# A two-layer decoder trunk on one core: the second layer's p projection in the convolution's end, attention's end on TensorE in a written order

## The chip, the core and the metric

The kernel runs on one core of one Trainium2 chip. The core has five engines that run side by side and wait for one another through semaphores: TensorE (PE, matmuls; PEld is its weight load), VectorE (DVE), ScalarE (ACT), GpSimd (POOL), and SyncE (SP, which here only issues transfers). PE writes its results to PSUM, eight banks of 128 x 512 float32. The metric is the device time of one execution in microseconds (us). Durations of single steps come from the trace of one profiled execution.

## What is computed

A trunk of two layers over 512 tokens of width 1024, all in float32. Layer 0 has a causal Conformer convolution, layer 1 differential attention with 8 heads; each is followed by a SwiGLU feed-forward and by a gated embedding of its own input p (256 features per layer):

```python
for i in range(DEPTH):                      # DEPTH = 2
    if i % N_MIXERS == 0:
        u = rms_norm(h, conv_norm_g[j])
        h = h + conformer_conv(u, ...)      # pw1, gate, 31 depthwise taps, layer norm, silu, pw2
    else:
        u = rms_norm(h, attn_norm_g[j])
        h = h + diff_attention(u, ...)      # heads' outputs, normalised, @ w_o
    u = rms_norm(h, ffn_norm_g[i])
    h = h + swiglu(u, ffn_w_gate[i], ffn_w_up[i], ffn_w_down[i])
    gate = jax.nn.sigmoid(rms_norm(h, ple_norm_g[i]) @ ple_w_gate[i])
    h = h + gate * (p[i] @ ple_w_proj[i])
```

The product `p[i] @ ple_w_proj[i]` depends on the inputs alone: it can be computed at any time before the last line of its layer. `w_o` is a 1024 x 1024 matrix: each of its eight output chunks sums over the eight heads.

## The kernel before

**Layout.** Activations lie as eight chunks of 128 channels by 512 tokens (`h[0]` to `h[7]`). Each float32 product is made from three matmuls of operands that are split into a high and a low part (`mm3`, L161: low x high, high x low, high x high). A weight tile is 128 x 1024: `weight()` (L145) loads it on SP's queue into the ring `wraw` (two buffers), ACT makes the high part `whi` (L156), DVE the low part `wlo` (L158); `whi` and `wlo` have four buffers each. PSUM has three rings: `mm` (four banks), `sc` (two), `tp` (two).

**Who sets the order.** A scheduler orders the instructions of each engine ahead of the run, by the order in which the program names them and by its own model of time; then each engine runs its list in order. `tc.issue_after(x)` keeps the instructions of a block behind x if they are on x's engine. Within `tc.manual_schedule(engines=...)` the named engines keep the order in which the program is written.

**The convolution's end (L482 to L544).** After the last chunk's taps (L482), `moments` (L415) squares the chunks y[5], y[6] and y[7] on ACT (L424) and adds them up on DVE or POOL (L428, L430). `project` (L269) makes one chunk of the first layer's p projection: six matmuls into an `mm` bank and a copy by ACT (L275). `factor` (L490) calls it: four chunks behind the last tap, then the sums over channels on PE (`add_moments`, L432, narrow matmuls L436 and wide ones L437), two chunks, then the row of scales (L513 to L522: DVE, POOL, ACT, PE), two chunks. With the scales each y is normalised (L539), passed through silu (L540) and split (L542, L544) for the matrix pw2 (`linear`, L546 and L571), whose first three weights are loaded in this time.

**Attention's end (L1015 to L1080).** The work of head hd and block qb of 128 queries is cut into three stages: `stage_s` (scores on PE, L944, L945; minimum, exponential and the difference of the two softmaxes on DVE and ACT, L947 to L956), `stage_t` (transposes on PE, L964, split L966, L967) and `stage_a` (product with the values, L980, L981; with the head's last block the head's normalisation, L987 to L1002). They stand in the list `stages`: in turn n, the score stage of unit n, the transposes of unit n - 2, the product of unit n - 3. 63 of the 96 stages are given out between the matmuls of the q, k and v slabs (L1028); 33 are left. `unit_end` (L896) transposes the last q and k block for the last two heads. `stage_o` (L1006) transposes a finished head and splits it (`split_scaled`, L177 and L178) into `ot[hd]`.

Then the second layer's features are loaded and split (`pfeatures`, L257 and L1055), its projection is computed with a stage from the list after each half chunk (L1057 to L1068), and the output matrix follows with further stages between (L1080): `linear` takes each chunk over all eight heads, the first two chunks side by side, `heads_until` (L1070) giving out stages until the head that is next is done. `add_attn` (L1076) adds a finished chunk to h and prepares it for the feed-forward (`Norm.chunk`: split L177 and L178, square L196, sum on POOL L197).

Of the kernel before, what the change touches and what calls it, by code (L numbers as in the profile page):

```python
# [12 lines left out]
F32 = mybir.dt.float32  # L13
F32R = mybir.dt.float32r
# [6 lines left out]
P = 128  # L21
S = 512
# [50 lines left out]
HALVES = slice(0, DH), slice(DH, P)  # L73
LT = 2
LA = 3
SQ_ACT = True
# [15 lines left out]
def trunk(ctx, tc, xT, pT, wts, diag, dww, vec, rel, onehot, lamv, out):  # L92
# [77 lines left out]
    def both(t):  # L170
        return t[:, 0], t[:, 1]
# [85 lines left out]
    def pfeatures(layer, parts):  # L257
        for k, (hi, lo) in enumerate(parts):
            raw = sb([P, 1024], "wraw", 2)[:, :S]
            nc.sync.dma_start(raw, pT[layer, :, k * S : (k + 1) * S])  # L260
            A.copy(hi, raw)
            (G if layer == 0 else V).tensor_tensor(lo, raw, f(hi), ALU.subtract)
# [4 lines left out]
    last_product = [None]  # L267

    def project(ph, m, w, o, step=lambda: None):  # L269
# [5 lines left out]
        A.copy(o, acc)  # L275
        return o
# [162 lines left out]
    for c in range(NC):  # L439
# [9 lines left out]
        if c > 0:  # L449
# [33 lines left out]
    other_taps(NC - 1)  # L483
    for c in range(NC - 3, NC):
        moments(c)


    pp = []

    def factor(after):  # L490
        m = len(pp)
        if m < 6:
            o = sb([P, S], f"D{m}", 1)
        elif m == 6:
            pw.append(sb([P, 2, S], "C4", 2))
            o = pw[2][:, 0]
        else:
            o = pw[2][:, 1]
        with tc.issue_after(after[0].ins):
            pp.append(project(ph, m, pw[m // 4], o))  # L500

    pw = [weight(), weight()]
# [18 lines left out]
    with tc.issue_after(last_product[0].ins):  # L521
        last_product[0] = T.matmul(lrow, ones, dg, start=True, stop=True)  # L522
    for _ in range(2):
        factor(last_product)
    with tc.issue_after(last_pow[0].ins):
# [502 lines left out]
    for what, at, pace in QKV:  # L1028
        ws = slab(GLO if at > 0 else 0)
        for tb in range(4):  # L1030
# [7 lines left out]
            else:  # L1038
                waiting = unit(at, ws, tb, between)
    unit_end(*waiting)  # L1040


    done = [0]

    def step():
        if stages:
            n, s = stages.pop(0)
            s()
        else:
            n = 99  # L1050
        while done[0] < NH and (n - LA - 3) // 4 > done[0]:
            stage_o(done[0])
            done[0] += 1

    ph = pfeatures(1, [both(sb([P, 2, S], t, 2, F32R)) for t in ("C0", "C1")])  # L1055
    pp = []
    for m in range(NC):  # L1057
        if m % 4 == 0:
            w = weight()
        step()  # L1060
        if m < 2:
            o = sb([P, S], f"D{m + 2}", 1)
        elif m % 2 == 0:
            o2 = sb([P, 2, S], f"C{m // 2 + 1}", 2)
            o = o2[:, 0]
        else:
            o = o2[:, 1]
        pp.append(project(ph, m, w, o, step))  # L1068

    def heads_until(k):  # L1070
        while done[0] <= k:
            step()

# [5 lines left out]

    linear(NC, ot, add_attn, 2, heads_until, step)  # L1080
    n2 = Norm("ple_g1")
# [34 lines left out]
def _layout(a):  # L1116
# [20 lines left out]

    tiles += proj(0)
    tiles += list(_stationary(a["conv_w_pw2"][0]))
    tiles += ffn(0)  # L1140
    tiles += list(_stationary(a["ple_w_gate"][0]))
    qkv = a["attn_w_qkv"][0]
    for what, at, _ in QKV:
# [7 lines left out]
        tiles += list(_moving(slab))  # L1151
    tiles += proj(1)
    tiles += list(_stationary(a["attn_w_o"][0]))
# [61 lines left out]
```

## Time and profile before

| | us |
|---|---|
| median of three executions | 1282.84 |
| the three executions | 1288.49, 1282.84, 1282.57 |
| the profiled execution's own time | 1285.64 |
| its span in the trace | 1283.8 |

| stage in the profiled execution | from, us | to, us |
|---|---|---|
| last taps end, first projection begins | 148.08 | |
| pw2's matmuls run without a break | 178.48 | |
| last tokens' matmul of q, k and v begins | 790.34 | |
| last score stage's minimum ends on DVE | | 833.66 |
| output matrix: last addition into h begins | 885.24 | |

How to read the profile: the page gives each engine's busy time over the span; a view by windows gives the same for chosen stretches, with the clock that PE was granted (1.00 is full) and the share of DMA; a timeline lists one engine's instructions by start and duration, with the idle time before an instruction and what ended it in brackets (`[1.04 <-DVE C L917]`: 1.04 us idle, ended by the instruction of L917 on DVE that writes the tile C). L158 is line 158 of the kernel. A busy PE can run at half clock, so the clock's column belongs to every statement about PE.

### The profile page before, as it was taken

The page shows a single profiled execution, that of the slowest core. Times are in us where ns is not written, and L with a number is a line of the kernel's source. Part 1 is how long each engine was busy: PE and PEld are TensorE (multiplying, and loading weights), DVE is VectorE, ACT ScalarE, POOL GpSimd, SP SyncE. Part 2 cuts the span into 40 slices and gives each one's busy share as a digit, 9 for nine tenths or more (in the row PEclk, how much of TensorE's full clock was granted, in tenths as well). Part 3 has the DMA queues.
Part 4 walks back from the last instruction along what each step waited for, and adds up shares of the span by engine and source line. Part 5 has one row for each costly group of instructions (what it writes and reads, how often), then busy time and mean ns, then how long its engine had stood idle before and what let it go on. Part 6 is the DMA issues. An engine that isn't in the chain of part 4 may idle for free. (4 is left out here: it accounts for less than half of the span.)

```text
span 1283.8 us, 18407 instructions
## 1 busy us (share of the span) xinstructions
PE 1253.2 (98%) x7056; PEld 1089.0 (85%) x7056; DVE 910.9 (71%) x1470; ACT 614.0 (48%) x1019; POOL 273.5 (21%) x239
## 2 busy tenths in 40 slices
PE   8999899999999999999999998999999999999998
PEld 5888678889899989988788886778888899899887
DVE  6888646785578557776678897946974588558665
ACT  5542445443255325454566766834542355235442
POOL 4645323000000000033335544122000001000030
PEclk8999989999999999999999999999999999999999
DMA  6654313275457545233222221313364466444241
GB/s 236 223 163 158 114 48 115 70 209 142 117 143 187 151 119 137 70 121 101 77 92 87 85 76 51 94 49 120 118 169 139 122 176 173 138 110 118 79 140 66
DMA packets 60164, 157.32 MB, mean 123 GB/s; under 512 B 6403, under 2 KB 11011, under 8 KB 60076
## 3 DMA queue, kind: packets, MB, share of 16 engines
q1 hardware_dynamic: 53344, 135.94, 33.2%
q0 software_dynamic: 4608, 16.78, 8.0%
q10 hardware_dynamic: 2124, 3.43, 0.9%
q8 instruction: 55, 0.90, 0.3%
q14 instruction: 33, 0.27, 0.1%
HBM read 151.91 MB, written 4.21 MB: 122 GB/s over the span
## 5 line engine op out<-in xcount | busy, mean ns | idle before, releaser
L164 PE MATMUL mm<-A,whi 128*128 128x512 f32 (+1 forms) x904 | 312.7, 347 | 0.6 <-DVE A L178 0.3
L163 PE MATMUL mm<-A,wlo 128*128 128x512 f32 (+1 forms) x904 | 308.3, 346 | 4.5 <-DVE wlo L158 2.5
L165 PE MATMUL mm<-A,whi 128*128 128x512 f32 (+1 forms) x904 | 310.0, 344 | 0.0
L156 ACT CAST whi<-wraw 128x1024 fp32r<-128x1024 f32 (+2 forms) x150 | 151.2, 1014 | 233.0 <-PE mm L165 93.4
L158 DVE TENSOR_TENSOR wlo<-wraw,whi 128x1024 fp32r<-128x1024 f32 (+2 forms) x146 | 186.6, 1280 | 65.8 <-ACT whi L156 65.0
L163 PEld LDWEIGHTS mm<-A,wlo 128*128 128x128 f32 x904 | 171.8, 190 | 27.5 <-DVE wlo L158 4.2
L164 PEld LDWEIGHTS mm<-A,whi 128*128 128x128 f32 x904 | 172.1, 190 | 24.5 <-DVE A L178 3.8
L165 PEld LDWEIGHTS mm<-A,whi 128*128 128x128 f32 x904 | 172.1, 190 | 20.4 <-issue 1.0
L164 PE MATMUL mm<-B,whi 128*128 128x512 f32 x352 | 137.3, 391 | 0.0
L650 POOL DMA_DIRECT2D C<-in_wts x32 | 28.1, 880 | 511.4 <-DVE h L761 179.4
L165 PE MATMUL mm<-B,whi 128*128 128x512 f32 x352 | 137.1, 390 | 0.0
L163 PE MATMUL mm<-B,wlo 128*128 128x512 f32 x352 | 134.9, 392 | 0.0
L197 POOL TENSOR_TENSOR acc<-acc,wk 128x512 f32<-128x512 f32 x42 | 65.7, 1564 | 229.6 <-ACT wk L196 122.1
L761 DVE TENSOR_TENSOR h<-mm,h 128x512 f32<-128x512 f32 x48 | 33.0, 687 | 64.8 <-PE mm L165 64.8
L165 PEld LDWEIGHTS mm<-B,whi 128*128 128x128 f32 x352 | 66.1, 188 | 14.4
L163 PEld LDWEIGHTS mm<-B,wlo 128*128 128x128 f32 x352 | 66.1, 188 | 14.0
L164 PEld LDWEIGHTS mm<-B,whi 128*128 128x128 f32 x352 | 66.1, 188 | 13.9
L165 PE MATMUL mm<-whi,A 128*128 128x512 f32 x192 | 75.7, 395 | 0.0
L164 PE MATMUL mm<-wlo,A 128*128 128x512 f32 x192 | 74.9, 395 | 0.0
L163 PE MATMUL mm<-whi,A 128*128 128x512 f32 x192 | 74.8, 396 | 0.0
L222 POOL TENSOR_TENSOR r<-v,mhalf 128x8 f32<-128x8 f32 (+1 forms) x31 | 46.2, 1490 | 117.1 <-DVE v L220 94.6
L643 DVE TENSOR_TENSOR wlo<-wraw,whi 128x1024 fp32r<-128x1024 f32 x32 | 39.2, 1225 | 32.8 <-ACT whi L642 32.8
(269 smaller groups left out, 2700.7 us busy)
## 6 DMA issues: line engine op xcount, KB each, us to landing
wraw<-in_wts SPq DMA_DIRECT2D x162, 512.0 KB, 3.7
C<-in_wts SPq DMA_DIRECT2D x32, 512.0 KB, 4.7
C<-in_wts POOLq DMA_DIRECT2D x32, 512.0 KB, 6.2
bias<-in_wts SPq DMA_DIRECT2D x32, 256.0 KB, 3.8
wraw<-in_wts SPq DMA_DIRECT2D x16, 384.0 KB, 3.1
D<-in_diag SPq DMA_DIRECT2D x22, 256.0 KB, 4.2
C<-in_diag SPq DMA_DIRECT2D x16, 256.0 KB, 4.4
h<-in_xT SPq DMA_DIRECT2D x8, 256.0 KB, 5.2
```

The source lines that it names most:

```text
L156: A.copy(hi[:, cut], raw[:, cut])
L158: eng.tensor_tensor(lo[:, cut], raw[:, cut], f(hi[:, cut]), ALU.subtract)
L163: T.matmul(acc, al, bh, start=first, stop=False)
L164: T.matmul(acc, ah, bl, start=False, stop=False)
L165: return T.matmul(acc, ah, bh, start=False, stop=last)
L197: self.last = self.eng.tensor_tensor(self.acc, self.acc, sq, ALU.add)
L222: last_pow[0] = G.tensor_tensor(r[:, :n], v[:, :n], mhalf[:, :n], ALU.pow)
L643: V.tensor_tensor(lo, raw, f(hi), ALU.subtract)
L650: nc.gpsimd.dma_start(q, wts[i + 2].rearrange("p (a s) -> p a s", a=2), accum_op=ALU.add)
L761: V.tensor_tensor(h[m], acc, h[m], ALU.add)
```

## The change

It has two parts.

**The second layer's p projection moves into the convolution's end.** At the fourth chunk of the convolution (c == 3) the second layer's features are loaded and split, their low parts on POOL, into the buffers `bias` and `C4`. `factor` gets a second list: eight more chunks, of the second layer, whose results go from a `big` buffer to device memory through ACT's queue (`kept`). The order on PE becomes: six chunks of the first layer, one of the second, the moments, four of the second, the row of scales, three of the second, the last two of the first. The squares of y[6] and y[7] are kept behind the copies of the fourth and sixth chunk on ACT (`last_copy`). Before the second layer's gated embedding the eight kept chunks are loaded back on SP's queue.

**Attention's end is written out for PE.** The last `unit_end` and all that follows stand in a `manual_schedule` block for PE. `step()` gives out one stage, and in every third call at most one `stage_o`. `filling()` is the first pass of the output matrix: for each chunk the four products with heads 0 to 3, one product (three matmuls) after each stage, then an addition into h. Nine stages come before `unit_end` (`AHEAD`). When the stages are used up, the rest of the first pass runs, then the second pass over heads 4 to 7: six chunks side by side in four `mm` and two `sc` banks for heads 4, 5 and 6, then head 7 for each of them with `add_attn`, then the last two chunks. `two_halves` loads the weights of two chunks for four heads as one 128 x 1024 tile.

The diff, cut to its core:

```diff
-            (G if layer == 0 else V).tensor_tensor(lo, raw, f(hi), ALU.subtract)
+            G.tensor_tensor(lo, raw, f(hi), ALU.subtract)
...
+        if c == 3:
+            ph1 = pfeatures(1, [[sb([P, S], "bias", 2, F32R) for _ in range(2)], both(sb([P, 2, S], "C4", 2, F32R))])
...
-    for c in range(NC - 3, NC):
-        moments(c)
+    moments(NC - 3)
...
+        with tc.issue_after(after.ins):
+            project(ph1 if second else ph, m, (pw1 if second else pw)[m // 4], o)
+        if second:
+            kept = dram.tile([P, S], F32, tag=f"pp{m}", name=f"pp{m}")
+            nc.scalar.dma_start(kept, o)
+            o = kept
+        made.append(o)
...
+    pw, pw1 = [[weight(), weight()] for _ in range(2)]
     for _ in range(4):
-        factor(last_tap)
+        factor(last_tap[0])
+    with tc.issue_after(last_copy[0].ins):
+        moments(NC - 2)
+    for _ in range(2):
+        factor(last_product[0])
+    with tc.issue_after(last_copy[0].ins):
+        moments(NC - 1)
+    factor(last_product[0], True)
     with tc.issue_after(last_product[0].ins):
         add_moments(y[NC - 1], sums["sq"], True, False)
         add_moments(macc, sums["acc"], False, True)
-    for _ in range(2):
-        factor(last_moment)
+    for _ in range(4):
+        factor(last_moment[0], True)
...
+    for _ in range(3):
+        factor(last_product[0], True)
     for _ in range(2):
-        factor(last_product)
+        factor(last_product[0])
...
-    unit_end(*waiting)
...
-        while done[0] < NH and (n - LA - 3) // 4 > done[0]:
+        count[0] += 1
+        if done[0] < NH and (n - LA - 3) // 4 > done[0] and count[0] % 3 == 2:
             stage_o(done[0])
             done[0] += 1
...
+    def filling():
+        for m in range(NC):
+            if m % 2 == 0:
+                two = two_halves(m, 0)
+            w = two[m % 2]
+            acc = mm()
+            for k in range(4):
+                while done[0] <= k:
+                    yield
+                mm3(acc, wpart(w, k), ot[k], k == 0, k == 3)
+                if k == 3:
+                    V.tensor_tensor(h[m], acc, h[m], ALU.add)
+                yield
+
+    fill = filling()
+    with tc.manual_schedule(engines={T.engine}):
+        for _ in range(AHEAD):
+            step()
+            next(fill)
+        unit_end(*waiting)
+        while stages:
+            step()
+            next(fill, None)
+        for _ in fill:
+            step()
+        while done[0] < 7:
+            step()
+        ws = [w for m in range(0, 6, 2) for w in two_halves(m, S)]
+        accs = [mm() for _ in range(4)] + [sc() for _ in range(2)]
+        for w, acc in zip(ws, accs):
+            for k in range(3):
+                mm3(acc, wpart(w, k), ot[4 + k], k == 0, False)
+        while done[0] < NH:
+            step()
+        for m, (w, acc) in enumerate(zip(ws, accs)):
+            mm3(acc, wpart(w, 3), ot[7], False, True)
+            add_attn(m, acc)
+        for m, w in zip((6, 7), two_halves(6, S)):
+            acc = mm()
+            for k in range(4):
+                mm3(acc, wpart(w, k), ot[4 + k], k == 0, k == 3)
+            add_attn(m, acc)
...
-    linear(NC, ot, add_attn, 2, heads_until, step)
```

The weights' order in memory follows: the second layer's two projection tiles now stand behind the first layer's.

More of the change, by code (lines that the diff above doesn't have):

```diff
@@ L274, in project @@
             step()
-        A.copy(o, acc)
+        last_copy[0] = A.copy(o, acc)
         return o
@@ L1048, in step, with add_attn @@
             s()
[L1049 to L1051 removed]
+        count[0] += 1
+        if done[0] < NH and (n - LA - 3) // 4 > done[0] and count[0] % 3 == 2:
             stage_o(done[0])
             done[0] += 1
[L1055 removed]
+    norm = Norm("ffn_g1")
+    def add_attn(m, acc):
+        V.tensor_tensor(h[m], acc, h[m], ALU.add)
+        norm.chunk(m)
+    base = wnext[0]
@@ new lines, in trunk, with two_halves @@
+    wnext[0] += NC
+    def two_halves(m, first):
+        raw = sb([P, 2, S], "wraw", 2)
+        nc.sync.dma_start(raw, bass.AP(wts.tensor, wts.offset + (base + m) * P * 1024 + first, [[1024, P], [P * 1024, 2], [1, S]]))
+        raw = raw.rearrange("p a s -> p (a s)")
+        hi = sb([P, 1024], "whi", 4, F32R)
+        lo = sb([P, 1024], "wlo", 4, F32R)
+        A.copy(hi, raw)
+        V.tensor_tensor(lo, raw, f(hi), ALU.subtract)
+        return [tuple(t[:, k * S : (k + 1) * S] for t in (hi, lo)) for k in range(2)]
@@ L1064, in trunk @@
             o2 = sb([P, 2, S], f"C{m // 2 + 1}", 2)
[L1065 to L1072, printed above, removed]
-    norm = Norm("ffn_g1")
-    def add_attn(m, acc):
-        V.tensor_tensor(h[m], acc, h[m], ALU.add)
-        norm.chunk(m)
-    linear(NC, ot, add_attn, 2, heads_until, step)
+        if m >= 2:
+            o = o2[:, m % 2]
+        nc.sync.dma_start(o, later[m])
+        pp.append(o)
     n2 = Norm("ple_g1")
```

31 lines of the change are left out of this document (17 added, 14 removed).

## The prediction

> **What bounds the kernel now.** I read the page's table of engines first. One core, so there is one span.
>
> ```profile
> PE 1253.2 (98%) x7056; PEld 1089.0 (85%) x7056; DVE 910.9 (71%) x1470; ACT 614.0 (48%) x1019; POOL 273.5 (21%) x239
> ```
>
> TensorE (PE) is busy for 1253.2 of 1283.8 us. The change computes the same matmuls, so it can win only idle PE time (30.6 us in all) and time in which PE runs at a lower clock. Next I read the table by windows over the two stages that the change touches: the convolution's end (first four rows) and attention's end up to the output matrix's last matmul (last four; 849 to 862 is left out). Its columns are busy time and instructions of each engine, then clock, DMA share and GB/s.
>
> ```profile
> 125.60:148.00 22.40, 22.31 (x123) 17.25 (x122) 11.40 (x16) 10.16 (x15) 7.41 (x7) 1.00 0.52 164
> 148.00:158.70 10.70, 7.44 (x26) 5.30 (x25) 9.33 (x13) 2.61 (x5) 5.29 (x5) 0.84 0.16 49
> 158.70:168.20 9.50, 9.50 (x37) 7.95 (x37) 0.97 (x5) 2.24 (x4) 0.02 (x1) 0.50 0.20 55
> 168.20:178.50 10.30, 9.52 (x31) 6.45 (x29) 6.00 (x8) 6.32 (x13) 7.28 (x6) 0.80 0.00 0
> ...
> 791.40:803.50 12.10, 5.86 (x28) 4.62 (x27) 11.83 (x32) 9.37 (x22) 4.53 (x5) 0.73 0.34 110
> 803.50:826.00 22.50, 20.57 (x110) 16.90 (x108) 21.05 (x58) 18.38 (x44) 4.10 (x5) 0.92 0.44 129
> 826.00:849.00 23.00, 22.79 (x135) 19.83 (x134) 13.63 (x40) 10.65 (x26) 3.89 (x4) 1.00 0.11 36
> ...
> 862.00:885.00 23.00, 23.00 (x102) 19.00 (x103) 14.98 (x15) 12.69 (x18) 9.51 (x6) 1.00 0.52 160
> ```
>
> Two things to see. From 158.7 to 168.2 PE is 9.50 of 9.50 us busy, but at a granted clock of 0.50: that "busy" hides half a stall. And from 791.4 to 826 VectorE (DVE) is busy 11.83 + 21.05 of 34.6 us, 95%, while PE idles: there DVE sets the pace, so PE's idle time can't all be had by reordering PE. Last I read PE's timeline for the idle time in attention's end.
>
> ```profile
> 793.74 0.63 PE L899 MATMUL tp<-ident,big 128*128 128x128 f32 x4 [1.04 <-DVE C L917]
> 795.19 0.30 PE L944 MATMUL sc<-C,C 128*128 128x128 f32 x1 [0.82 <-DVE st L947]
> 797.92 0.47 PE L944 MATMUL sc<-C,C 128*128 128x128 f32 x1 [1.65 <-DVE st L947]
> 801.13 0.66 PE L944 MATMUL sc<-C,C 128*128 128x384 f32 x1 [2.52 <-DVE st L955]
> 811.77 0.44 PE L944 MATMUL sc<-C,C 128*128 128x384 f32 x1 [0.81 <-DVE st L947]
> 815.27 0.47 PE L944 MATMUL sc<-C,C 128*128 128x512 f32 x1 [0.94 <-DVE st L947]
> 857.13 1.20 PE L163 MATMUL mm<-A,wlo 128*128 128x512 f32 x4 [0.78 <-ACT A L177]
> 861.90 0.50 PE L163 MATMUL mm<-A,wlo 128*128 128x512 f32 x1 [1.75 <-DVE wlo L158]
> ```
>
> These waits add up to 10.3 us, all on DVE or ACT results. PE had nothing else there: the weights of projection and output matrix are issued only from 796.62 on, when the features' splits (L262) have let go of the load ring.
>
> ```profile
> 796.62 15.12 SPq L153 DMA_DIRECT2D wraw<-in_wts  x6
> ```
>
> **The change, part by part.** *Price of a matmul.* The second and third of the next rows are 16 matmuls apart, so one 128x512 matmul costs (152.37 - 148.71) / 16 = 0.229 us at full clock. The second layer's projection is 8 chunks of 6, 48 matmuls: 11.0 us. The output matrix is 8 x 8 x 3 = 192 matmuls, 44 us, in either kernel.
>
> ```profile
> 148.08 0.80 PE L163 MATMUL mm<-wth,wlo 128*128 128x512 f32 x1
> 148.71 0.39 PE L164 MATMUL mm<-wth,whi 128*128 128x512 f32 x1
> ...
> 152.37 0.39 PE L165 MATMUL mm<-wtl,whi 128*128 128x512 f32 x1
> 156.01 0.79 PE L163 MATMUL mm<-wth,wlo 128*128 128x512 f32 x1 [3.26 <-ACT D L275]
> 158.74 1.73 PE L436 MATMUL tp<-ones,wk 128*128 128x1 f32 x8
> ...
> 168.22 1.42 PE L163 MATMUL mm<-wth,wlo 128*128 128x512 f32 x1
> ...
> 172.41 0.40 PE L165 MATMUL mm<-wth,whi 128*128 128x512 f32 x1
> ...
> 173.33 1.02 PE L522 MATMUL tp<-wk,ones 128*128 128x512 f32 x2
> ...
> 178.48 0.50 PE L163 MATMUL mm<-A,wlo 128*128 128x512 f32 x1 [0.78 <-DVE wlo L158]
> ```
>
> *Convolution's end, 148.1 to 178.0 us* (two matmuls of the next layer ran before 178.48). Now: three projection chunks, 3.26 us idle, two chunks, the moments at half clock (158.74 to 168.2), two chunks of which the clock recovers in the second, the row of scales, two chunks. The 3.26 us is ACT's queue: a copy of a finished chunk stands behind a square that waits for y. The change puts the copies ahead of the squares (`last_copy`), so that wait goes. Dense, 16 chunks cost 16 x 6 x 0.229 = 22.0 us. The moments' price at full clock is not shown there; the nearest rows are the norm's own sums and spread:
>
> ```profile
> 900.78 0.86 PE tp L237 x2
> ...
> 1241.82 0.79 PE tp L203 x8
> ```
>
> Eight small ones 0.79 us against 1.73 at half clock, a wide pair 0.86 us against 2.05: 4 x 0.8 + 2 x 0.86 = 4.9 us for 32 small and two wide pairs, where 9.5 us are spent now. With the scales' row 0.9 us that is 27.8 us: PE could reach the next layer at 148.1 + 27.8 = 175.9, 2.1 us sooner than now with 11 us more work in it. That is the lower end.
>
> What is late next is the second weight of the first projection, needed from the fifth chunk on, which the change puts ahead of the moments. In the present order its low half comes on DVE right behind y's last addition:
>
> ```profile
> 157.19 0.69 DVE L404 TENSOR_TENSOR B<-mm,B 128x512 f32<-128x512 f32 x1
> 157.79 1.22 DVE L158 TENSOR_TENSOR wlo<-wraw,whi 128x1024 fp32r<-128x1024 f32 x1
> ```
>
> The change moves two DVE additions (L428, L430; 0.6 us each) behind it, so it would end at 159.0 - 1.2 = 157.8. PE has four chunks until 148.1 + 5.5 = 153.6 and then waits 4.2 us. After such a wait the clock is half until some 4 us of dense matmuls have run (168.22 to 172.41): three chunks then take 4.1 + 2.0 = 6.1 us, to 163.9; moments 168.8; four chunks (5.5) 174.3; scales 175.2; five chunks (6.9) 182.1, against 178.0: 4 us slower. If the moments run at half clock too, 4.6 us more and about 1.5 behind them: 10 us slower, the upper end. The scales' chain lies beside four chunks (5.5 us) in any case: its first and last steps now lie 169.24 + 1.27 - 167.33 = 3.2 us apart.
>
> ```profile
> 167.33 0.17 DVE L513 TENSOR_SCALAR v<-tp 128x8 f32<-128x8 f32 x1 [8.32 <-PE tp L436]
> ...
> 155.39 0.57 ACT L275 COPY D<-mm 128x512 f32<-128x512 f32 x1
> ...
> 169.24 1.27 ACT L519 ACTIVATE wk<-ident,r 128x128 f32<-128x128 f32 x4 [8.30 <-POOL r L222]
> ```
>
> The two added low halves (2 x 1.22) fall where DVE has 0.97 us of work in 9.5; eight more ACT copies (0.57 each) and eight stores on ACT's queue lie in ACT's idle time there; they cost nothing while a copy (0.57) is shorter than a chunk (1.37), else up to a chunk each. Loading the features in the convolution's middle takes two buffers of the weight ring and two POOL subtractions: 0, or a few us of delay in a weight that comes a whole chunk ahead. Between -2 and +10 I take **+3 us**, nearest to the row at 157.79.
>
> [...]
>
> *Attention's end, 791.4 to 885.0 us*, 93.5 us. Lost now: the 10.3 us of waits and about 3 us at half clock (0.73 and 0.92 in the first two windows). Without them and without the projection's 11.0, PE needs 93.5 - 13.3 - 11.0 = 69.2 us: a gain of 24.3 if nothing waits. But DVE:
>
> ```profile
> L158 DVE TENSOR_TENSOR wlo<-wraw,whi 128x1024 fp32r<-128x1024 f32 x7 | 8.8, 1261 | 0.7 <-ACT whi L156 0.7
> L178 DVE SCALAR_TENSOR_TENSOR A<-tp,lam,A 128x512 fp32r<-128x512 f32 x8 | 6.0, 748 | 4.9 <-ACT A L177 4.9
> ...
> L1077 DVE TENSOR_TENSOR h<-mm,h 128x512 f32<-128x512 f32 x4 | 2.6, 684 | 1.0 <-PE mm L165 1.0
> ...
> L262 DVE TENSOR_TENSOR C<-wraw,C 128x512 fp32r<-128x512 f32 x2 | 1.4, 680 | 0.0
> ```
>
> From 791.4 to 849 it works 46.5 us. Gone: the features 1.4 and two projection weights 2.4. (A split of L178's kind, 0.75 us, is needed again for each finished chunk.) New before the second pass: eight additions of the first pass into h, 8 x 0.68 = 5.4, and three weights more, 3.6. That is 51.7 us, of which some 2 us (the last head's small operations) lie beside the second pass. At the 95% that DVE reaches now, 50 us take 53, so the second pass starts near 791.4 + 53 = 844.5. PE's own work until there is 69.2 - 21.9 = 47 us, so DVE sets this stage. The last head's normalisation then stands in PE's written order only five output steps (5 x 0.69 us) and one other head's transposes behind its last product. From that product to its transposes it now takes 855.76 - 848.79 = 7 us, which other matmuls fill, so some 2 us of wait come: 846.5.
>
> ```profile
> 848.79 0.22 PE L981 MATMUL mm<-B,wtl 128*128 128x128 f32 x1
> ...
> 855.76 0.60 PE L1009 MATMUL tp<-ident,D 128*128 128x128 f32 x4
> ```
>
> Second pass: 32 x 3 x 0.229 = 22.0, to 868.5. There six chunks finish within 4.1 us and put 6 x (0.68 + 0.75) = 8.6 us on DVE, so the next layer's first weights may come 2 us late: 870.5 against 885.0, **-14.5 us**. Loading the eight kept products needs no PE; it is 2 MB on SP's queue where DMA is 11% busy or idle, behind the output matrix's weights; cost 0, or a weight's landing (4.2 us) if a buffer holds the queue.
>
> Sum: +3 - 14.5 = -11.5 us. The profiled execution took 1285.64 us (span 1283.8), so 1274 by its own time; the median of the three is 2.8 lower. Forecast **1271.5 us**.
>
> **The rivals.**
> 1. *Dense.* The second weight lands in DVE's idle time before 148 (11.40 of 22.40 us busy): conv -2, attention -18 or better: 1263. For: DVE is idle there. Against: the row at 157.79.
> 2. *Moved, not hidden.* The clock stays half through the moments: conv +10, attention -14.5: 1278. For: clock 0.50 now. That the projection isn't hidden at all is this case at its end.
> 3. *Slower: the written order.* Each of the 33 steps left (score, transpose or product) is followed on PE by an output step in program order, and four of these stand right behind the transposes that feed them. If every step waits as PE does at 797.92 or 793.74 (1.65, 1.04), say 1.1 us, the tail takes 69.2 + 36 = 105 us, 11.8 more than now, and with +3: 1297. It decides from (24.3 - 3) / 33 = 0.65 us a step on. For: DVE is 95% busy, and the present order can pass a waiting step. Against: the waits overlap DVE work that must be done anyway. [...]
>
> **How the numbers follow.** A measurement of this kernel can tell about 0.5% (6.4 us) from no change. Forecast (1266 to 1277) 0.47; dense 0.20; moved 0.21; slower 0.12. Faster by over 0.5% (under 1276.4): 0.45 + 0.20 + 0.05 = 0.70; slower (over 1289.3) 0.09; the same 0.21. The range leaves out the slower rival and the best tenth: 1258 to 1283.
>
> **What would show it.** Clock in the convolution's end: 1.00 through the moments (rival 1), half behind a wait at the fifth chunk (forecast), half to the end (2). DVE over 90% busy from the last tokens' matmul to the second pass, and the pass 53 to 55 us after it; over 65 us means rival 3. PE's waits in attention's end 3 to 9 us. It would be wrong if the scheduler, which still orders DVE and ACT, puts a second-pass weight or a feature load where it holds PE in order.

## The result and the profile after

The changed kernel takes **1296.67 us** (median of four executions, 1294.31 to 1298.10); four executions of the kernel before beside it have a median of 1285.12 us. The ratio is 1.0086, 95% interval 1.0064 to 1.0108: about 0.9% slower. Forecast was 1271.5 us, so neither the sign nor the range held.

The page's table of engines, changed kernel (profiled execution 1298.10 us, the longest of the four; span 1296.3):

```profile
PE 1255.5 (97%) x7056; PEld 1091.8 (84%) x7056; DVE 912.1 (70%) x1476; ACT 615.9 (48%) x1019; POOL 280.4 (22%) x241
```

PE runs the same 7056 matmuls and is busy 2.3 us longer, in a span that is 12.5 us longer: some 10 us are new idle time. Three marks that both kernels have tell where it arose: the projection's first matmul, the last tokens' matmul of q, k and v, and the start of the output matrix's last addition into h.

| | before | after | added |
|---|---|---|---|
| projection in the convolution's end begins | 148.08 | 154.78 | +6.7 |
| last tokens' matmul begins | 790.34 | 798.30 | +8.0 (1.3 more) |
| last addition into h begins | 885.24 | 897.33 | +12.1 (4.1 more) |
| span | 1283.8 | 1296.3 | +12.5 (0.4 more) |

So in this trace the stages up to the last tokens lost 8.0 us, all of it in the convolution (pw2's matmuls begin 8.1 us later, at 186.62), and attention's end takes 99.0 us instead of 94.9 although 11 us of matmuls have left it. First the convolution's front, in PE's timeline of the changed kernel:

```profile
86.50 5.78 PE L354 MATMUL sc<-C,D 128*128 128x128 f32 x36 [4.46 <-DMA C<-pi]
...
154.78 0.79 PE L164 MATMUL mm<-wth,wlo 128*128 128x512 f32 x1
```

PE stands idle for 4.46 us before a block of shifted taps, until the transfer of the shifted copies (C<-pi) lands; before it was 1.37 us. After that wait the 36 small matmuls take 5.78 us instead of 4.25, at a granted clock of 0.73. A later block of taps loses 2.6 us in the same way (1.98 us idle and 5.88 us at a clock of 0.71; before, 1.00 and 4.26 us at 1.00). Next the convolution's end by windows (columns as in the prediction):

```profile
154.78:164.78 10.00, 10.00 (x44) 7.78 (x42) 6.38 (x8) 5.43 (x9) 0.00 (x0) 1.00 0.02 7
164.78:174.60 9.82, 9.82 (x43) 7.75 (x43) 1.18 (x5) 2.34 (x6) 1.51 (x2) 0.67 0.23 80
174.60:186.62 12.02, 12.02 (x51) 9.53 (x50) 7.13 (x10) 8.29 (x14) 5.80 (x5) 0.98 0.57 183
```

PE is never idle there. Seven chunks run at full clock (1.00), the first half of the moments too (1.00 from 164.78 to 168.00), then the clock drops (0.53 from there to 171.27, 0.67 over the window). From the first projection to pw2's matmuls it takes 186.62 - 154.78 = 31.8 us, against 30.4 before (178.48 - 148.08): most of the projection's 11 us did find room. Last, attention's end by windows, from the last tokens' matmul on:

```profile
798.00:823.00 25.00, 13.93 (x58) 10.07 (x56) 19.32 (x49) 14.33 (x35) 7.39 (x8) 0.66 0.43 140
823.00:848.00 25.00, 18.95 (x90) 15.48 (x91) 17.24 (x50) 11.66 (x29) 2.84 (x4) 0.86 0.18 54
848.00:872.00 24.00, 21.09 (x120) 17.55 (x119) 17.02 (x46) 10.83 (x24) 3.95 (x4) 1.00 0.19 55
872.00:897.00 25.00, 24.79 (x111) 20.58 (x112) 12.93 (x16) 11.51 (x18) 5.75 (x5) 1.00 0.22 62
sum 99.00, PE 78.76 PEld 63.69 DVE 66.51 ACT 48.33 POOL 19.93; mean PE 19.69 PEld 15.92 DVE 16.63 ACT 12.08 POOL 4.98
```

In the first 50 us PE is busy for 33 and its clock is 0.66 and 0.86; DVE, which the prediction had at 95% there, is busy for 36.6 of 50 us. So neither is at its limit: they wait for each other. The view of waits names for whom PE waits from 798 to 873 (us in all, times, longest):

```profile
PE mm L165 <- DVE A L179: 4.2, 3, 2.4
PE sc L964 <- DVE st L967: 3.9, 4, 1.3
PE mm L164 <- ACT A L178: 3.7, 4, 1.4
PE tp L1029 <- DVE wtl L987: 3.6, 1, 3.6
PE tp L1029 <- POOL D L1022: 2.1, 1, 2.1
PE tp L919 <- DVE C L937: 1.7, 1, 1.7
PE tp L984 <- DVE v L221: 1.0, 1, 1.0
```

Together 20.2 us, twice the 10.3 of before. The first and third row, 7.9 us, are output steps that stand right behind the transposes of the head they use, and wait for its split on ACT and DVE.

### The profile page after: what moved, and what is told of

Same layout as the page of the kernel before. It is cut to its first block, busy times and chain, and to the rows that moved or that the text cites. A ratio compares the mean times of both kernels' runs of the same rounds, so it can differ in the third digit from the quotient of the medians.

```text
span 1296.3 us, 18431 instructions
## 1 busy us (share of the span) xinstructions
PE 1255.5 (97%) x7056; PEld 1091.8 (84%) x7056; DVE 912.1 (70%) x1476; ACT 615.9 (48%) x1019; POOL 280.4 (22%) x241
## 4 chain that ended last, share of the span: by engine, by line
PE 81%; DVE 9%; DMA 3%; ACT 3%; issue 2%; POOL 1%; SPq 1%; ACTq 0%; DVEq 0%; POOLq 0%
PE mm L165 21%; PE mm L164 21%; PE mm L166 21%; PE tp L166 2%; PE tp L165 2%; PE tp L164 2%; PE sc L354 2%; DVE wlo L159 1%; PE sc L165 1%; PE sc L166 1%; PE sc L164 1%; DMA wraw<-in_wts 1%; DVE A L179 1%; DMA C<-pi 1%; PE mm L1000 1%
## 5 line engine op out<-in xcount | busy, mean ns | idle before, releaser
L157 ACT CAST whi<-wraw 128x1024 fp32r<-128x1024 f32 (+2 forms) x142 | 142.7, 1012 | 237.2 <-PE mm L166 113.5
L159 DVE TENSOR_TENSOR wlo<-wraw,whi 128x1024 fp32r<-128x1024 f32 (+2 forms) x138 | 174.0, 1263 | 67.8 <-ACT whi L157 67.4
L391 POOL TENSOR_TENSOR wk<-wk,C 128x512 f32<-128x512 f32 x36 | 55.0, 1528 | 26.7 <-ACT C L390 24.9
```

The costliest lines, as they stand in the source:

```text
L157: A.copy(hi[:, cut], raw[:, cut])
L159: eng.tensor_tensor(lo[:, cut], raw[:, cut], f(hi[:, cut]), ALU.subtract)
L391: G.tensor_tensor(pacc, pacc, pr, ALU.add)
```

## The experiments

Two questions: is the written order what costs in attention's end (theory W), or DVE and the heads' chain whatever PE's order (D)? And do the features' loads cost the front its 6.7 us (R)? This table has every run; the rows of before and after come first. "Tail" is last tokens' matmul to last addition, "rest" last addition to the span's end, all from one profiled execution each. The ratio is to the kernel before, run beside it.

| run | median, us | ratio, 95% interval | projection begins | last tokens | tail | rest |
|---|---|---|---|---|---|---|
| before | 1285.12 | | 148.1 | 790.3 | 94.9 | 398.6 |
| after | 1296.67 | 1.0086 (1.0064 to 1.0108) | 154.8 | 798.3 | 99.0 | 399.0 |
| e1 features early | 1302.61 | 1.0144 (1.0124 to 1.0165) | 158.5 | 802.8 | 99.2 | 398.6 |
| e2 tail scheduled | 1285.62 | 1.0007 (0.9994 to 1.0021) | 154.4 | 798.2 | 85.7 | 401.7 |
| e3 heads three later | 1292.37 | 1.0057 (1.0034 to 1.0080) | 157.1 | 797.7 | 95.9 | 398.1 |
| e4 convolution alone | 1289.83 | 1.0045 (1.0028 to 1.0062) | 153.6 | 794.7 | 94.9 | 398.4 |
| e5 features late | 1298.52 | 1.0104 (1.0077 to 1.0132) | 149.2 | 795.2 | 100.6 | 398.4 |
| e6 both mended | 1289.23 | 1.0029 (1.0013 to 1.0045) | 153.5 | 799.5 | 85.3 | 401.5 |
| e7 two passes alone | 1284.58 | 0.9987 (0.9972 to 1.0002) | 149.4 | 787.9 | 96.2 | 398.5 |
| e8 no steps ahead | 1299.95 | 1.0116 (1.0087 to 1.0144) | 152.8 | 793.8 | 104.7 | 398.2 |
| e9 halves on POOL | 1282.03 | 0.9979 (0.9961 to 0.9996) | 151.9 | 800.1 | 85.3 | 401.4 |
| e10 half after y | 1288.76 | 1.0026 (1.0011 to 1.0042) | 149.7 | 802.9 | 84.7 | 398.5 |
| e11 tail scheduled, halves on POOL | 1284.02 | 0.9994 (0.9980 to 1.0007) | 153.4 | 794.3 | 85.4 | 402.3 |
| e12 as e9, again | 1283.54 | 0.9972 (0.9955 to 0.9989) | 148.3 | 796.3 | 85.4 | 403.3 |

### Attention's end: e2, e3, e8, e4, e7

**e2: the same tail in the scheduler's order.**

```diff
-    with tc.manual_schedule(engines={T.engine}):
+    with nullcontext():
```

> The changed kernel with its tail (last stages of attention, two passes of the output matrix) left to the scheduler's order on TensorE instead of the written one; two passes and the moved projection stay. Theory W (the written order makes PE wait for heads and tile banks that are just being made: 15.0 us of waits and half clock between 799 and 833): the tail, 98.8 us in the changed kernel, falls to 84 to 88 us, time 1282 to 1287. Rival D (the tail is set by DVE and by the chain through the last heads, whatever PE's order): tail 95.5 us or more, time within 3 us of the changed kernel (1293 to 1298).

The time is 1285.62 us, 11 us below the changed kernel, and the tail 85.7 us: W. Windows of e2, over the same first 50 us as above, and the sum of its four windows up to 884:

```profile
798.00:823.00 25.00, 18.74 (x99) 15.14 (x97) 22.21 (x60) 17.94 (x44) 7.72 (x9) 0.86 0.44 151
823.00:848.00 25.00, 22.87 (x124) 18.68 (x125) 24.33 (x68) 15.56 (x38) 2.81 (x3) 1.00 0.23 74
...
sum 86.00, PE 76.83 PEld 62.65 DVE 67.17 ACT 49.63 POOL 21.82; mean PE 19.21 PEld 15.66 DVE 16.79 ACT 12.41 POOL 5.46
```

With the same instructions DVE now works 46.5 of 50 us (93%), PE 41.6, and PE's waits up to 862 are down to 8.2 us, the largest of them these:

```profile
PE tp L1029 <- DVE wtl L987: 1.7, 1, 1.7
PE tp L919 <- DVE C L937: 1.7, 1, 1.7
PE mm L1000 <- ACT wth L986: 1.4, 3, 0.8
PE sc L964 <- DVE st L967: 1.3, 2, 0.8
```

Over the whole stage PE is idle for 20.2 us in the changed kernel (99.00 less 78.76) and for 9.2 in e2 (86.00 less 76.83): 11 of the 13.3 us that the tail is shorter. In the other 2 the same matmuls are busy for less time, at a higher clock (0.86 and 1.00 in the first 50 us instead of 0.66 and 0.86). Six traces have this tail in the scheduler's order (e2, e6, e9 to e12 in the table), and it takes 84.7 to 85.7 us in all of them. Some of the gain is given back later: the rest of the program takes 401.7 us instead of 399.0. PE's timeline of e2 has one new wait there, in the feed-forward, and a clock of 0.68 in the 5.4 us behind it:

```profile
952.65 0.39 PE L164 MATMUL mm<-A,wlo 128*128 128x256 f32 x1 [2.69 <-DVE wlo L663]
```

**e3: the written order, with each output step three steps behind its head.**

```diff
-                while done[0] <= k:
+                while past[-4] <= k:
                     yield
```

(`past` holds `done[0]` as it stood after each step.)

> The changed kernel with the written order kept, but an output step may use a head only three steps after that head was transposed (at present in the same step). Theory W, in the form that the waits on the split of a head just transposed are the price (about 7 us of the 15.0, and the half clock behind them): those waits are gone from PE's groups of weight high times head low and high times high (4.7 us idle behind the split now), time 5 to 10 us below the changed kernel (1286 to 1291). Theory D, or W in the form that the waits on the tile banks and on the last q chain decide: the time moves by at most 3 us (1293 to 1299).

1292.37 us, 4.3 below the changed kernel: just under the range of W's first form, just over the bound of the other. The tail is 95.9, 3.1 shorter. The waits of e3 (from 798 to 870):

```profile
PE sc L964 <- DVE st L967: 3.7, 3, 2.4
PE tp L1029 <- DVE wtl L987: 3.6, 1, 3.6
PE tp L1029 <- POOL D L1022: 3.4, 1, 3.4
PE tp L984 <- DVE C L937: 2.7, 2, 1.8
PE sc L964 <- DVE v L1017: 2.0, 1, 2.0
PE tp L919 <- DVE C L937: 1.7, 1, 1.7
```

The 7.9 us on heads just split are gone, as meant; but with two small rows that are not shown (0.8) the sum is still 17.9. PE now stops at scores, banks and transposes that it used to reach later. In this fixed order the waits that were taken away at one place came back, for the most part, at the next.

**e8: no output steps ahead of the last pair's transposes.**

```diff
-AHEAD = 9
+AHEAD = 0
```

> The changed kernel with no output steps ahead of the last pair's transposes (nine now); the written order stays. Theory A (the nine steps hold the last pair's q and k, issued 27 us after the last token instead of 11, so the last heads' whole chain is late): the last pair's transposes 15 to 20 us earlier, the second pass 4 to 8 us earlier, time 1289 to 1293. Rival B (the waits of single steps on heads just transposed and on tile banks are the price; with fewer output steps in the first stages they grow): time within 3 us of the changed kernel or above it (1294 to 1301).

1299.95 us and a tail of 104.7, 5.7 longer: theory A falls, and the time lies in rival B's range. The last pair's transposes do come earlier (806.59 instead of 826.39), but PE then has nothing in its order to do while POOL makes their operand (waits of e8, from 794 to 875):

```profile
PE tp L919 <- POOL big L913: 7.7, 1, 7.7
PE mm L164 <- ACT A L178: 3.8, 4, 1.5
```

The nine steps ahead hid more than they cost.

**e4: the new convolution's end with the old tail, without the projection.** The tail block is the one of before (`unit_end`, `step`, `linear`), less the projection; the kept products are loaded back. The lines show the tail against the kernel before.

```diff
-    ph = pfeatures(1, [both(sb([P, 2, S], t, 2, F32R)) for t in ("C0", "C1")])
...
-        pp.append(project(ph, m, w, o, step))
...
     linear(NC, ot, add_attn, 2, heads_until, step)
```

> The convolution's end of the changed kernel alone: the second layer's projection there, its products stored and loaded back; attention's end as before the change (scheduler's order on PE, one pass over the heads), without the projection. The front stays 8 us behind the kernel before (798.5 instead of 790.6 where the last tokens end). Theory W (the new order of the tail eats what the projection's absence gives): the old tail of 94.6 us loses the projection's 11 us, up to 14 with its clock, so 81 to 84 us, and the time is 1279 to 1283. Theory D (that tail is bound by DVE and its waits; the projection only filled holes): tail 91 to 95 us, time 1289 to 1294.

1289.83 us, inside D's range, and the tail is 94.9 us, the same as before to a tenth, with 11 us of matmuls less. The windows of e4, whose tail begins at 794.72:

```profile
795.00:820.00 25.00, 14.60 (x59) 11.30 (x58) 21.04 (x55) 15.07 (x36) 8.24 (x10) 0.66 0.47 147
820.00:845.00 25.00, 21.03 (x121) 17.43 (x119) 19.02 (x66) 14.05 (x39) 4.33 (x4) 0.89 0.10 32
845.00:867.00 22.00, 19.48 (x99) 16.00 (x98) 9.11 (x18) 7.85 (x14) 2.67 (x3) 0.97 0.00 1
```

PE is idle for 10.4, 4.0 and 2.5 us in them. In the one-pass tail the projection had cost nothing: it was what PE did while the heads were made. Summed from the last tokens' matmul to the last addition, PE's idle time grows from 10.9 us (before) to 16.9 without the projection. Its busy time falls by only 6.0 us, from 84.0 to 78.0, since the clock is lower too (0.66 in the first 25 us instead of 0.80). The mechanism is read from these sums; what the run itself shows is that the tail did not get shorter. For this tail D was right.

With the tail and the rest unchanged, e4 also prices the new convolution, with the features' loads and the kept products, by medians: 1289.83 against 1284.88 beside it, 5.0 us. The 8.0 us of the changed kernel come from the trace of its longest execution; e4's own trace has 4.4 (794.72 against 790.34).

**e7: the kernel before with the two passes alone** (heads 0 to 3 added into h, then heads 4 to 7 as in the change), the projection still in the tail, the scheduler's order.

```diff
-    linear(NC, ot, add_attn, 2, heads_until, step)
+    for m in range(NC):
...
+                V.tensor_tensor(h[m], acc, h[m], ALU.add)
+            step()
+    heads_until(6)
...
```

> The kernel before with only the output matrix's two passes (first pass added into h, scheduler's order); the projection stays in the tail and the convolution's end as before. Theory F (the projection filled holes of the one-pass tail: leaving it out gave 94.6 us against 94.7; two passes fill the same holes, so its 11 us count again): tail 95 to 99 us, time 1285 to 1289, no gain. Rival T (two passes gain by themselves what the scheduled tail of the changed kernel gains, 6 us, and moving the projection gains nothing): tail 87 to 90 us, time 1278 to 1280.

Tail 96.2, 1284.58 us against 1285.15 beside it: no gain. (The time falls 0.4 below the range named, the tail inside it; rival T, 87 to 90, is out.) So the four tails that the scheduler orders are: one pass with the projection 94.9, one pass without it 94.9, two passes with it 96.2, two passes without it 85.7. Neither edit gains alone. The sums by windows say where the 10.5 us between the last two lie: PE is idle for 9.2 us in e7 (96.2 less 87.0 busy) and for 9.2 in e2 (85.7 less 76.5). So all of it is busy time, the price of the projection's matmuls. The first pass is a second filler; only when there are two is it worth taking one out. One thing was not tested by itself: e2 also names its stages in another order than e7 (nine steps ahead of `unit_end`, one `stage_o` in three calls). The equal idle time speaks against a large part for it.

### The convolution: e1, e5, e6, e9 to e12

**e1: features loaded at the start of the program,** behind the first layer's.

```diff
+    ph1 = pfeatures(1, [[sb([P, S], "bias", 2, F32R) for _ in range(2)], both(sb([P, 2, S], "C4", 2, F32R))])
...
-        if c == 3:
-            ph1 = pfeatures(1, [[sb([P, S], "bias", 2, F32R) for _ in range(2)], both(sb([P, 2, S], "C4", 2, F32R))])
```

> The changed kernel with the second layer's features loaded right behind the first layer's, as before the change, and not in the convolution's middle; all else is changed. Theory R (the two feature loads in the convolution's middle hold the weight ring and SP's queue, so that the shifted copies of the image part come late and PE waits for them ahead of the third and fourth group of taps): the wait of 4.46 us on that transfer falls back to about 1.4 us, the projection starts near 148 us of the span instead of 154.8, and the time is 6 to 7 us below the changed kernel (about 1290). Rival P (the taps stand in another order in the changed kernel for another reason, and the loads cost nothing): projection starts at 154 to 155, time within 1.5 us of the changed kernel (1296 to 1298).

1302.61 us, worse, which neither theory expected. PE's timeline of e1:

```profile
33.90 0.80 PE L164 MATMUL mm<-A,wlo 128*128 128x512 f32 x1 [5.41 <-DVE wlo L159]
...
92.92 4.25 PE L355 MATMUL sc<-C,D 128*128 128x128 f32 x36 [0.57 <-DMA C<-pi]
```

At this block the wait on the shifted copies shrinks from 4.46 to 0.57 us and the taps run at full clock, as R said; a later block still waits 3.33 us (124.05; 1.98 in the changed kernel). And the two loads now hold the ring of weights at the start: the weights that were issued at 20.46 are issued at 25.78, and the convolution's first matmul behind the norm stands at 33.90 instead of 26.48. The test moved the price instead of removing it.

**e5: features late,** issued between the first and the second layer's projection weights.

```diff
-    pw, pw1 = [[weight(), weight()] for _ in range(2)]
+    pw = [weight(), weight()]
+    ph1 = pfeatures(1, [[sb([P, S], "bias", 2, F32R) for _ in range(2)], both(sb([P, 2, S], "C4", 2, F32R))])
+    pw1 = [weight(), weight()]
```

> The changed kernel with the second layer's two feature loads issued in the program between the first and the second layer's projection weights (the convolution's end) instead of at the fourth of its eight steps; the written tail stays. Ahead of the second and third block of shifted taps TensorE then has 268 and 366 other matmuls in program order, as in the kernel before, against 257 and 353 in the changed kernel. Theory R2 (the loads' place in the middle made the scheduler put the taps 11 and 13 matmuls earlier, ahead of the transfer that they need, so that PE waits and then runs at half clock): projection starts at 147.5 to 149.5 us of the span instead of 154.8, time 6 to 7 us below the changed kernel (1289 to 1291). Rival L (late features only move the wait to the seventh chunk of the projection, which needs them): projection starts at 148 but the next layer at 184 or later, time within 3 us of the changed kernel.

Half of R2 is shown: with the old order of taps the projection begins at 149.24 in place of 154.78. But the time does not follow (1298.52; its four executions lie at 1296.0, 1296.1, 1301.0 and 1302.1, and the trace is of the first). PE's timeline of e5:

```profile
86.79 4.25 PE L354 MATMUL sc<-C,D 128*128 128x128 f32 x36 [1.83 <-DMA C<-pi]
...
149.24 0.79 PE L164 MATMUL mm<-wth,wlo 128*128 128x512 f32 x1
160.60 0.80 PE L164 MATMUL mm<-wth,wlo 128*128 128x512 f32 x1 [3.97 <-DVE B L406]
```

Part of what PE gains in front it loses at the projection's sixth chunk, which needs the bank that y's last addition (L406) reads; the clock is 0.64 over the 4.25 us behind that wait. The addition starts at 159.85 in e5 and at 159.82 in the changed kernel; before, it was at 157.19. Of the 5.5 us, 2.4 are gone when pw2's matmuls begin (183.48 instead of 186.62), and 3.1 are left at the last tokens. This is in part rival L's outcome at another place: not the features but y's chain on DVE ends last here. It does not explain the median: the trace is of one of the two short executions, and no trace shows what the other two, 5 us longer, do.

Over all runs: with the features in the middle (after, e2, e3, e4, e8, e11) PE waits 4.06 to 5.36 us at that block of taps, in the eight other traces 0.57 to 3.12. The projection begins at 154.3 on average in this group (152.8 to 157.1), with late features (e5, e6, e9, e10, e12) at 150.5 (148.3 to 153.5). The last tokens' matmul stands at 796.2 in the first group (793.8 to 798.3), at 798.8 in the second (795.2 to 802.9), at 790.3 and 787.9 in the two kernels with the old convolution. So the earlier start is not seen there. All five kernels with late features wait 3.97 to 4.32 us within the projection, four of them for y's last addition and e10 for a weight's low half; the first group waits 0.6 us or less.

**e6: both edits, e2 and e5 together.**

> Features as in the run with late features, and the tail left to the scheduler (two passes, no written order). If the two causes are separate, the gains add: 1285.6 less 6 to 7, so 1278.5 to 1280.5, faster than the kernel before by about 5 us. If one hides the other (the front's gain is lost in a later wait), 1283 to 1286.

1289.23 us, worse than e2 alone, and than either case expected. The two gains do not add. Up to attention's end this is e5's program, but in its trace the block of taps waits 2.60 us and then runs at a clock of 0.71 (e5: 1.83 us, 1.00), and the projection begins 4.3 us later than in e5, at 153.51. Then PE waits 3.97 us again for y's last addition, which comes at 164.1.

**e9, e11, e12: the low halves of the four projection weights on POOL;** e9 and e12 on top of e6, e11 on top of e2. DVE's timeline of the changed kernel shows what the edit is aimed at:

```profile
139.54 1.21 DVE L159 TENSOR_TENSOR wlo<-wraw,whi 128x1024 fp32r<-128x1024 f32 x1
...
142.36 1.21 DVE L159 TENSOR_TENSOR wlo<-wraw,whi 128x1024 fp32r<-128x1024 f32 x1
143.50 0.75 DVE L401 SCALAR_TENSOR_TENSOR sc<-C,C,shrow 128x512 f32<-128x512 f32 x1
...
155.85 1.15 DVE L372 SCALAR_TENSOR_TENSOR B<-B,vec,shrow 128x512 f32<-128x512 f32 x1 [2.10 <-DMA B<-po]
```

Two of the halves stand ahead of the last chunk's thirteen taps, which begin at 143.50; in the kernel before they began at 141.49. In this trace they do not set the end of y's chain, though: between these taps and y's last addition DVE is idle for 2.10 us, until a transfer (B<-po) lands. In e5 and e6 it has no such wait there, and one half ahead of the taps takes 2.29 us.

```diff
-    pw = [weight(), weight()]
+    pw = [weight(eng=G), weight(eng=G)]
...
-    pw1 = [weight(), weight()]
+    pw1 = [weight(eng=G), weight(eng=G)]
```

> The kernel of both mends (late features, scheduled tail: 1289.2 us) with the low halves of the four projection weights subtracted on POOL instead of DVE. Theory Y (two of these halves, 1.2 us each, stand on DVE ahead of the last chunk's 13 taps; they make y's last addition 2.6 us later than in the kernel before, and the projection's sixth chunk waits 3.97 us for the bank that this addition reads): the addition comes 2 to 2.6 us sooner against the projection's start, the wait falls to 1 to 2 us, time 1286 to 1287. Rival P2 (POOL's own taps of the same chunk, 6.75 us to 155.6, are pushed back by two halves of some 2.6 us each and hold y instead): wait 3 to 6 us, time 1289 to 1292.

> The kernel with the scheduled tail (features in the convolution's middle, 1285.6 us) with the low halves of the four projection weights on POOL. Theory Y: 1283 to 1284.5, which would be the fastest of all by some 1 us, against 1285.1 before. Rival P2, or the front's late start (154.4) hides y's chain anyway: 1285 to 1287.

> The kernel with late features, scheduled tail and low halves on POOL a second time, because its profiled execution (1288.65 us) was the longest of its ten and shows y's last addition late, against a median of 1282.0. Theory Y (the median's gain is real and comes from y's chain): median 1281 to 1283.5, and an ordinary profiled execution has y's last addition at 157 to 158.5 us and the projection's wait behind it under 3 us. Rival P2 (y is as late as in that profile, and the 1282.0 was a draw): median 1285 to 1288, addition at 160 or later.

e9 took 1282.03 us, 7 below e6 and more than theory Y gave; e12, the same kernel, 1283.54 (at the edge of theory Y's range); e11 1284.02, 1.6 below e2 and within Y's range. e9 and e12 are the fastest kernels of this study, 0.2 to 0.3% below the kernel before, with both intervals under 1. Where it comes from the traces do not settle. POOL's, DVE's and PE's rows of e12, one fence for each:

```profile
135.91 2.35 POOL L159 TENSOR_TENSOR wlo<-wraw,whi 128x1024 fp32r<-128x1024 f32 x1 [8.82 <-ACT whi L157]
138.98 2.85 POOL L159 TENSOR_TENSOR wlo<-wraw,whi 128x1024 fp32r<-128x1024 f32 x1 [0.71 <-ACT whi L157]
```

```profile
157.80 0.69 DVE L406 TENSOR_TENSOR B<-mm,B 128x512 f32<-128x512 f32 x1
```

```profile
158.64 0.77 PE L164 MATMUL mm<-wth,wlo 128*128 128x512 f32 x1 [4.32 <-DVE B L406]
```

The addition stands at 157.80, as Y expected, but PE waits 4.32 us for it, not under 3. In e9's trace it is at 161.41 and PE waits 4.30 us, with POOL's own taps running until 158.6 as rival P2 said. Both profiled executions are among the longest of their kernel (1288.65 us, median 1282.03; 1286.77, median 1283.54), so what the ordinary ones do differently is in no trace here.

**e10: the second weight's low half behind y's last addition,** on top of e6, on DVE.

```diff
-    pw = [weight(), weight()]
+    pw = [weight(), weight(after=last_add[0])]
```

> The same kernel of both mends with the second projection weight's low half ordered behind y's last addition on DVE, as the kernel before had it (157.79). Theory Y: y's last addition comes 1.2 us sooner, but the projection's fifth chunk now waits for the half itself, some 1.2 us longer than for the bank: time 1288 to 1290, no gain. Rival: the bank's wait was all, the half is in time: 1287 to 1288.

1288.76 us, as theory Y expected: y's last addition comes at 157.98, and PE then waits 4.18 us for the half itself. Counted from the projection's start, the addition comes after 8.3 us, against 10.6 in e5 and e6. So by these single traces the half's place explains some 2.3 us of y's delay; the whole was not traced to one cause.

## Why the prediction was wrong

**The bound of the tail: right in one order, not in the one that runs.** The step that failed is "at the 95% that DVE reaches now, 50 us take 53", and with it "DVE sets this stage". It was meant to put the second pass 53 to 55 us behind the last tokens' matmul; the text named over 65 us as the sign of rival 3. In the changed kernel the last head's transposes, one output step ahead of the second pass, stand at 872.21, 73.9 us behind:

```profile
872.21 0.66 PE L1029 MATMUL tp<-ident,D 128*128 128x128 f32 x4 [2.13 <-POOL D L1022]
```

The amount of work was forecast well: DVE works 53.3 us up to the second pass (50 to 51.7 in the forecast). But it needs 75.1 us for them, 71% and not 95%. In e2, where the scheduler chooses, DVE is 93% busy in the first 50 us, and the second pass's first products in the `sc` banks run 58 us behind the last tokens:

```profile
856.29 0.39 PE L164 MATMUL sc<-A,wlo 128*128 128x512 f32 x1
```

The resource was named rightly; the forecast then took it for granted that PE's written order would deliver DVE's work on time.

**Rival 3, the written order, is what happened.** Priced at 1.1 us a step, deciding from 0.65. In the working's terms PE needs 69.2 us; the tail is 4.1 us longer than before's 93.5, so 97.6, and the loss is 28.4 us, 0.86 a step, over the point from which it decides. The waits (20.2 us) are twice the 10.3 of before and beyond the forecast's 3 to 9. The argument against it, "the waits overlap DVE work that must be done anyway", is refuted by DVE's 36.6 of 50 us. The chance of 0.12 was too small: 95% of one engine in an order that a scheduler made around the waits says nothing of an order written without them. That its time, 1297, matches the measured 1296.67 is luck: in the trace the tail lost 4.1 us where it said 11.8, the convolution 8.0 where it said 3.

**The bound of -24.3, and -14.5 of it taken.** Taking the projection out was counted as 11.0 us of PE's work saved. e4 shows 0.0 us in the one-pass tail, and e2 against e7 shows 10.5 us in the two-pass tail. Even in the scheduler's order the tail gains 9.2 us (94.9 to 85.7), of which the rest of the program gives back 3.1. The late first weight of the next layer, put at 2 us, came as 0.55 us in e2 and none in the changed kernel; the larger one, 2.69 us in the feed-forward, was not foreseen. It is not bound to this tail: in e10 it is 0.90 us, and the rest takes 398.5.

**The convolution's +3: near in its own stretch, and short of what came ahead of it.** Measured 8.0 us in the trace and 5.0 by e4's medians, both within the -2 to +10. But of the 8.0 us only 1.4 arose in the stretch for which the +3 was worked out (31.8 us against 30.4); 6.7 arose ahead of it, in the taps, which the forecast had at "0, or a few us".
- *The late second weight* did not come late: its low half ran at 142.36, in time for the fifth chunk. There it stands ahead of y's taps, and y's last addition moved from 157.19 to 159.82; in this trace DVE waits for a transfer in between, and PE has no idle time in the stretch, so the half is not shown to cost anything here. Where the projection begins sooner (e5, e6), PE does wait for y. The forecast had followed one instruction to the front of a queue and not asked whom it passes.
- *The features' load in the middle, cost "0, or a few us of delay in a weight"*: no weight came late, and the copies C<-pi did not either (PE goes on at 86.50; before 86.07, e5 86.79). The taps that need them stood 11 and 13 matmuls further forward in PE's order. Worth 6.7 us at the projection's start in this trace, 3.8 between the averages of the two groups of runs; but with late features y's chain, or in e10 a weight's low half, ends last instead.
- *The moments* took 6.5 us (164.78 to the next chunk at 171.27), between the 4.9 at full clock and the 9.5 of before; the clock fell half way. In e4 and e11 they run at full clock throughout (5.0 us in e4).
- *Stores, copies and loads of the kept products at no cost*: nothing in the changed kernel contradicts it; the rest of the program takes 399.0 us against 398.6.

## What to carry to other kernels

Before work is moved away, ask whether it was filling holes: if so it saves nothing where it leaves, and what it costs where it lands (here 5.0 us) is lost, unless another filler takes its place. An order written by hand for one engine is to be priced by its waits, step by step: here they came to 20.2 us, against 8.2 us for the same instructions in the scheduler's order (e2). A busy share measured in a scheduler's order is no evidence for it (DVE's 95% before, 36.6 of 50 us after). And an operation that is moved forward in one queue is to be charged with what it passes, where the chain behind it ends last (e5, e6); in the changed kernel itself that cost is not shown.

## What the runs showed of the hardware

In these runs the length of an idle gap alone did not decide whether the clock fell. The rows below are the same block of taps, from PE's timeline of e7 and then of e9:

```profile
86.93 5.88 PE L352 MATMUL sc<-C,D 128*128 128x128 f32 x36 [2.48 <-DMA C<-pi]
```

```profile
89.40 4.26 PE L354 MATMUL sc<-C,D 128*128 128x128 f32 x36 [3.12 <-DMA C<-pi]
```

After 2.48 us of idle time the 36 matmuls took 5.88 us, at a granted clock of 0.71, after 3.12 us 4.26, at 1.00. At the same block waits of 2.11 (e10) and 2.60 us (e6) were followed by 5.88 us too, waits of 1.54 (e12) and 1.83 us (e5) by 4.26 and 4.25. The prediction's "after such a wait the clock is half" was read from one place in the trace of before, 3.26 us of idle time and then a clock of 0.50 from 156.00 to 172.41; e9's 3.12 us with 1.00 behind them show that it does not hold for every wait of that length.

The same code began its projection at 148.1 in one kernel and 149.4 in another, and at 151.9 and 148.3 in the two traces of one kernel (e9, e12). Kernels that differ only in attention's end reached the last tokens between 793.8 and 798.3 us. A difference of 4 us between two single traces of this kernel is therefore no finding in itself.

A 128 x 1024 subtraction took 2.35 and 2.85 us on POOL (e12), 1.21 on DVE (both rows of the changed kernel).
